# Which FFN chunks are turned by VectorE and DMA, and which by TensorE: three and ten instead of nine and nine

## The chip, the core and the metric

The kernel runs on one core of one Trainium2 chip. The metric is the device time of one execution in microseconds (us). Before the change the median of three runs is 1899.93 us (1897.19 to 1902.32). Engines are named as in the profile: PE is the matrix engine (PEld its weight loads), DVE the vector engine, ACT the scalar engine, POOL the general engine, SP the engine whose queue issues most loads.

## What is computed

A decoder trunk of two layers over 256 tokens with 2048 features, all in 32-bit floats. Layer 0 mixes tokens by causal pooling, layer 1 by latent attention; each layer ends with a gated feed-forward network (FFN) with 5632 inner features. What matters here:

```python
def swiglu(h, w_gate, w_up, w_down):
    return (jax.nn.silu(h @ w_gate) * (h @ w_up)) @ w_down
...
        x = x + gate_m[:, None, :] * y
        h = modulate(rmsnorm(x, norm_ffn[i]), shift_f, scale_f)
        x = x + gate_f[:, None, :] * swiglu(h, ffn_gate[i], ffn_up[i], ffn_down[i])
```

## The kernel before

**Units.** Every weight matrix is cut into units of 512 by 512 (1 MB). A unit is loaded by SP into one of six `raw` buffers (L389), split by ACT into a rounded upper half (`hi`, L376) and by DVE into the rest (`lo = raw - hi`, L378), and multiplied by PE in 24 matmuls of 128x512 (L422): `hi` by both halves of the activations, `lo` by the upper half, for four slices of 128 rows and two tiles of 128 tokens. The halves lie in six `hl` buffers, so PE can be at most three units behind the splits. Matmuls accumulate in eight PSUM banks.

**An FFN.** The inner features are eleven chunks of 512. `project_chunk(c)` (p in the list below) multiplies the hidden state by the gate and up columns of chunk c; ACT takes the silu (L852), DVE multiplies (L856) into `nat[c]`, two tiles with tokens on the partitions. For the down projection the features of the chunk must lie on the partitions: `transposed(c)` (t) turns `nat[c]` into `mids[c]`, again as upper and lower half. `down(i)` (d) multiplies a group of two or three chunks by their rows of `w_down`. The order is written out by hand:

```python
FFN_STEPS = "p0 p1 t0 p2 t1 p3 t2 p4 p5 d0 t3 t4 p6 t5 d1 p7 t6 p8 t7 p9 t8 d2 p10 t9 d3".split()
GROUPS = ([0, 1, 2], [3, 4, 5], [6, 7, 8], [9, 10])
```

Three quarters of the gate and up products of chunks 0 to 5 are made ahead of these steps (`start_ffn`); their sums lie in SBUF, and DVE adds the last quarter from PSUM (L722).

**Two ways of turning.** A chunk below `TURNED_BY_DMA` = 9 is turned in blocks of 32: DVE turns 32x32 blocks within the tile (`turn_blocks`, L752), POOL writes the tile to DRAM (L754, 256 KB), `transposed` lets POOL read it back with the blocks in their places (L769), and then ACT and DVE make the halves from SBUF (`turned_halves`, L761 and L762). The rows of `w_down` are stored in the order that this leaves. A chunk from 9 on is turned by PE: four 128x128 transposes into a PSUM bank for each token tile (L777), and ACT and DVE make the halves from PSUM (L780, L781). In the last group the transposes of chunk 10 are issued inside the first unit of d3.

**Background.** During the first FFN, DVE also sums the modulation vectors of later stages: tiles of 1 MB are loaded into the same six `raw` buffers (L212) and reduced by DVE (L213), by a rate of about one tile per unit. When the sixteen tiles of one vector are summed, DVE writes the column (L302), and PE turns it (L294) for the gate of the FFN.

**Order on the engines.** A scheduler sets it when the program is built, from the order of the code and priorities (the splits stand a little ahead). On each engine instructions run in the order that it set, and an instruction that waits holds back what stands behind it. `pending` holds work that is issued in code order a unit or two later, behind the next splits.

Of the kernel before, what the change touches and what calls it, by code (L numbers as in the profile page):

```python
# [17 lines left out]
P = 128  # L18
# [4 lines left out]
CH = 512  # L23
ND = D // CH
F = 5632
NF = F // CH
DEPTH = 2
# [6 lines left out]
KL = LORA // P  # L34
# [23 lines left out]
FFN_STEPS = "p0 p1 t0 p2 t1 p3 t2 p4 p5 d0 t3 t4 p6 t5 d1 p7 t6 p8 t7 p9 t8 d2 p10 t9 d3".split()  # L58
GROUPS = ([0, 1, 2], [3, 4, 5], [6, 7, 8], [9, 10])
BLOCK = 32  # L60
TURNED_BY_DMA = 9

BEGUN = 6
ASIDE = 5
# [31 lines left out]
def tile_trunk(ctx: ExitStack, tc: tile.TileContext, a: dict, out: bass.AP):  # L96
# [19 lines left out]
    def act_t(shape, dt=F32R):  # L116
        return work.tile(shape, dt, tag="act", bufs=8, name=nm("act"))

    def t2k(shape, dt=F32):
        return work.tile(shape, dt, tag="t2k", bufs=7, name=nm("t2k"))  # L120
# [7 lines left out]
    def ps_t():  # L128
        return psum.tile([P, CH], F32, tag="ps", name=nm("ps"))
# [143 lines left out]
    pending = []  # L273
# [329 lines left out]
    def stream_aside(l):  # L603
        if l == 0:
            return
        aside[l] = dram.tile([P, NT, D], F32, name=nm("aside"))
        with tc.issue_after(w_load[0].ins):
            sync.dma_start(aside[l], x)
# [129 lines left out]
    def ffn(l, hT, gate_name, begun, then):  # L738
# [3 lines left out]
        def project(c, which):  # L742
            if c in begun:
                begun[c][which].block(ND - 1, hT[ND - 1])
                return begun[c][which].result()
            return proj(ffn_weights(l)[which][:, c], hT)

        def turn_blocks(c):
            turned[c] = []
            for tok in range(NT):  # L750
                blocks = t2k([P, CH])
                dve.transpose(out=blocks, in_=nat[c][tok])  # L752
                rows = dram.tile([P, CH], F32, name=nm("turned"))
                pool.dma_start(rows, blocks)  # L754
                turned[c].append(rows)

        def turned_halves(m, tok, full):
            order = "p k (b j) -> p k b j"
            v = full.rearrange("p (b k j) -> p k b j", k=KL, j=BLOCK)
            upper, lower = (m[:, i, :, tok * P:(tok + 1) * P].rearrange(order, j=BLOCK) for i in range(2))  # L760
            act.activation(upper, v, AF.Copy)  # L761
            dve.tensor_tensor(out=lower, in0=v, in1=upper.bitcast(F32), op=ALU.subtract)  # L762

        def transposed(c):
            m = act_t([P, 2, KL, T])
            if c < TURNED_BY_DMA:
                for tok in range(NT):
                    full = t2k([P, CH])
                    pool.dma_start(full.rearrange("p (b e) -> p b e", e=P),  # L769
                                   turned[c][tok].rearrange("(b i) (g e) -> (i g) b e", i=BLOCK, e=P))  # L770
                    pending.append((1, lambda tok=tok, full=full: turned_halves(m, tok, full)))
                mids[c] = m
                return
            for tok in range(NT):
                pt = ps_t()
                for f in range(KL):
                    pe.transpose(pt[:, f * P:(f + 1) * P], nat[c][tok][:, f * P:(f + 1) * P], ident)  # L777
                v = pt.rearrange("p (f t) -> p f t", f=KL)
                ts_ = slice(tok * P, (tok + 1) * P)
                act.activation(m[:, 0, :, ts_], v, AF.Copy)  # L780
                dve.tensor_tensor(out=m[:, 1, :, ts_], in0=v, in1=m[:, 0, :, ts_].bitcast(F32), op=ALU.subtract)  # L781
            mids[c] = m
# [9 lines left out]
        def down(i):  # L792
# [6 lines left out]
            for j in range(ND):  # L799
# [29 lines left out]
                for c in g:  # L829
                    hi, lo = w_unit(wd[c, j])  # L830
                    turning = last and j == 0 and c == g[0]
                    proj_unit(banks, mids[c], hi, lo, c == g[0], c == g[-1],
                              between=(lambda: transposed(g[-1])) if turning else None)
# [6 lines left out]
        def project_chunk(c):  # L840
            if c == ASIDE:
                stream_aside(l)
            if c == NF - 1:
                end = StreamEnd(l)
                stream_end.append(end)
                for n, wait in enumerate(KNOWN):
                    pending.append((wait, lambda n=n: end.known(n // NT, n % NT, gates[gate_name])))
            gb = project(c, GATE)
            nat[c] = []
            for tok in range(NT):  # L850
                sg = t2k([P, CH])
                pending.append((0, lambda sg=sg, bank=gb[tok]: act.activation(sg, bank, AF.Silu)))  # L852
                nat[c].append(sg)
            ub = project(c, UP)
            for tok in range(NT):
                dve.tensor_tensor(out=nat[c][tok], in0=ub[tok], in1=nat[c][tok], op=ALU.mult)  # L856
            if c < TURNED_BY_DMA:
                pending.append((0, lambda: turn_blocks(c)))

        for step in FFN_STEPS:  # L860
            {"p": project_chunk, "t": transposed, "d": down}[step[0]](int(step[1:]))
# [845 lines left out]
def units(w):  # L1707

    k, n = w.shape
    w = w.reshape(k // CH, KL, P, n // CH, CH).transpose(0, 3, 2, 1, 4)  # L1710
    return w.reshape(k // CH, n // CH, P, KL * CH)


def laid_out(i):

    def columns(v):
        return np.asarray(v).reshape(-1, P).T

    o = {n: np.asarray(i[n]) for n in ("x", "c", "positions", "mod_w", "final_norm")}
    o["vectors"] = np.concatenate([columns(i[n]) for n in (  # L1720
        "c", "norm_mix", "norm_ffn", "kv_in_norm", "kv_norm", "q_norm", "pool_scale", "mod_b", "kv_mod_b")], 1)
    o["mod_wt"] = o["mod_w"].transpose(0, 2, 1)
    o["kv_mod_wt"] = np.asarray(i["kv_mod_w"]).T
    block = o["mod_w"][0].reshape(KD // 2, 2, P, 6, D)[:, :, :, 3:5, :CH]
    o["mod_block"] = block.transpose(0, 2, 1, 3, 4).reshape(KD // 2, P, 4 * CH)

    w = np.asarray(i["w_uq"])[0].reshape(KL, P, H // 2, 2, QH)
    rope = w[..., NOPE:].reshape(KL, P, H // 2, 2, 2, HALF).swapaxes(3, 4).reshape(KL, P, H // 2, 2 * ROPE)
    w = np.concatenate([rope, w[..., :NOPE].reshape(KL, P, H // 2, 2 * NOPE)], 3)
    o["w_uq"] = w.transpose(2, 1, 0, 3).reshape(H // 2, P, -1)  # L1730
    w = np.asarray(i["w_kr"]).reshape(KD, P, 2, 1, HALF)
    o["w_kr"] = np.concatenate([w, w], 3).reshape(KD, P, P).transpose(1, 0, 2).reshape(P, KD * P)
    for n in ("w_dkv", "w_uk", "w_uv"):
        o[n] = units(np.asarray(i[n]))
    o["pool_w"] = np.asarray(i["pool_w"])[0].reshape(-1, KL, P, CH).transpose(0, 2, 1, 3).reshape(-1, P, KL * CH)
    for n in ("w_dq", "w_o"):
        o[n] = units(np.asarray(i[n])[0])
    for n in ("ffn_gate", "ffn_up", "ffn_down"):
        o[n] = np.stack([units(w) for w in np.asarray(i[n])])
    w = np.asarray(i["ffn_down"]).reshape(DEPTH, NF, KL, KL, BLOCK, ND, CH)[:, :TURNED_BY_DMA]  # L1740
    o["ffn_down"][:, :TURNED_BY_DMA] = w.transpose(0, 1, 5, 4, 2, 3, 6).reshape(DEPTH, TURNED_BY_DMA, ND, P, KL * CH)
    return o


# [16 lines left out]
```

## Time and the profile before

| | |
|---|---|
| median of three runs | 1899.93 us (1897.19 to 1902.32) |
| profiled execution | 1897.58 us, span 1895.8 us |
| mean granted clock of PE | 0.992 |
| PE busy | 1833.5 us (97% of the span) |
| DVE busy | 1437.9 us (76%) |
| ACT busy | 835.9 us (44%) |
| DMA of SP's queue | 570.68 MB, 77.5% of 16 engines |
| DMA of POOL's queue | 22.02 MB, 3.1% of 16 engines |

The parts of the span, by PE's rows: the modulation vectors and the pooling mixer until 166 us, the first FFN until about 888 us (its `start_ffn` until about 362 us), the attention until about 1174 us, the last FFN to the end (1895.8 us). The span is counted from the first instruction to the last of the profiled execution; its own time is 1.8 us longer. A row of the timeline gives the start, the length, the engine, the line, the operation and, in brackets, how long the engine had been idle and what ended that.

### The profile page before, as it was taken

To read this page: it belongs to the slowest core of one execution; us is meant where nothing else is said; L and a number is where in the kernel's file an instruction comes from. 1 tells how busy PE (TensorE), PEld (TensorE's weight loads), DVE (VectorE), ACT (ScalarE), POOL (GpSimd) and SP (SyncE) were. 2 spreads that over 40 slices of the span, in tenths; PEclk is the share of its full clock that TensorE was granted. 3 is DMA by queue.
4 is the path that set the end of the run, shared out by engine and by line. 5 is a ranking of instruction groups with operands and counts; after the bars stand their busy time and mean duration, and the time that the engine had idled before them with its cause. 6 is when DMAs were issued, how large, how long until landed. Compare 5 with 4: busy or idle time off the path is not lost.

```text
span 1895.8 us, 21717 instructions
## 1 busy us (share of the span) xinstructions
PE 1833.5 (97%) x8589; PEld 1485.8 (78%) x8589; DVE 1437.9 (76%) x1447; ACT 835.9 (44%) x914; POOL 69.1 (4%) x102
## 2 busy tenths in 40 slices
PE   6689999998999999999999999999999999999998
PEld 2356888886888888888889888888888888888886
DVE  1248799999889798997798886889788666644557
ACT  3125643443443343344766635634444433344343
POOL 0000000010000000000100000000011000000000
PEclk9989999999999999999999999999999999999999
DMA  9999998899999899995494485989788776765551
GB/s 398 417 420 415 387 363 338 317 356 349 410 401 417 356 398 395 390 420 223 181 381 171 159 351 191 397 323 331 264 312 326 285 270 236 273 250 207 218 200 45
DMA packets 85879, 594.37 MB, mean 314 GB/s; under 512 B 10081, under 2 KB 10513, under 8 KB 17041
## 3 DMA queue, kind: packets, MB, share of 16 engines
q1 hardware_dynamic: 79346, 570.68, 77.5%
q0 software_dynamic: 6192, 22.02, 3.1%
q8 instruction: 67, 1.10, 0.2%
q10 hardware_dynamic: 240, 0.29, 0.0%
q14 instruction: 34, 0.28, 0.0%
HBM read 577.20 MB, written 15.75 MB: 313 GB/s over the span
## 4 chain that ended last, share of the span: by engine, by line
PE 88%; DMA 7%; DVE 3%; issue 1%; ACT 1%; SPq 0%; POOLq 0%; DVEq 0%; ACTq 0%
PE ps L422 76%; DMA raw<-in_mod_w_dram 6%; PE ps L431 2%; PE ps L1382 1%; DVE hl L378 1%; PE ps L258 1%; PE ps L1029 1%; PE ps L1468 1%; PE ps L1574 1%; DVE raw L213 1%; DMA raw<-in_ffn_down_dram 1%; PE ps L1285 1%; ACT hl L376 0%; DMA raw<-in_mod_block_dram 0%; PE ps L564 0%
## 5 line engine op out<-in xcount | busy, mean ns | idle before, releaser
L422 PE MATMUL ps<-hl,act 128*128 128x512 f32 x6672 | 1520.5, 390 | 4.1 <-ACT hl L376 3.3
L422 PEld LDWEIGHTS ps<-hl,act 128*128 128x128 f32 x6672 | 1252.5, 188 | 265.6 <-ACT hl L376 4.4
L376 ACT ACTIVATE hl<-raw 128x2048 fp32r<-128x2048 f32 x285 | 546.1, 1917 | 671.0 <-PE ps L422 397.1
L378 DVE TENSOR_TENSOR hl<-raw,hl 128x2048 fp32r<-128x2048 f32 x285 | 651.3, 2287 | 200.9 <-ACT hl L376 198.9
L213 DVE SCALAR_TENSOR_TENSOR raw<-raw,s_row 128x2048 f32<-128x2048 f32 x168 | 383.0, 2284 | 12.9 <-DMA raw<-in_mod_wt_dram 12.1
L258 PE MATMUL ps<-raw,s_strip 128*32 128x512 f32 x392 | 58.9, 686 | 39.3 <-DMA raw<-in_mod_w_dram 38.1
L722 DVE TENSOR_TENSOR act<-ps,act 128x512 f32<-128x512 f32 x96 | 63.8, 681 | 14.7 <-PE ps L422 14.7
L258 PEld LDWEIGHTS ps<-raw,s_strip 128*32 128x32 f32 x392 | 8.9, 116 | 69.6 <-DMA raw<-in_mod_w_dram 48.7
L754 POOL DMA_DIRECT2D turned<-t2k x36 | 20.1, 561 | 800.3 <-DVE t2k L752 799.9
L431 PE MATMUL ps<-hl,act 128*128 128x512 f32 x192 | 47.6, 400 | 0.6 <-DVE act L527 0.5
L431 PEld LDWEIGHTS ps<-hl,act 128*128 128x128 f32 x192 | 35.1, 188 | 10.3 <-ACT act L514 2.5
L790 DVE TENSOR_TENSOR x<-ps,x 128x512 f32<-128x512 f32 x32 | 21.5, 688 | 19.9 <-PE ps L422 19.9
L769 POOL DMA_DIRECT2D t2k<-turned x36 | 27.5, 764 | 222.1 <-issue 106.2
L544 DVE TENSOR_TENSOR hl<-raw,hl 128x2048 fp32r<-128x2048 f32 (+3 forms) x17 | 31.9, 1879 | 4.8 <-ACT hl L541 4.7
L265 DVE COPY t2k<-ps 128x256 f32<-128x256 f32 x4 | 1.7, 424 | 44.0 <-ACT t2k L264 44.0
L856 DVE TENSOR_TENSOR t2k<-ps,t2k 128x512 f32<-128x512 f32 x24 | 16.5, 688 | 23.6 <-PE ps L422 23.6
L1029 PEld LDWEIGHTS ps<-act,act 128*128 128x128 f32 x128 | 24.0, 194 | 11.3 <-issue 8.4
L451 ACT ACTIVATE junk<-x 128x512 bf16<-128x512 f32 x23 | 14.4, 628 | 41.0 <-DVE x L636 23.9
L720 ACT ACTIVATE act<-ps 128x512 f32<-128x512 f32 x32 | 19.1, 596 | 29.0 <-PE ps L422 29.0
L1029 PE MATMUL ps<-act,act 128*128 128x256 f32 x128 | 30.9, 392 | 0.0
L752 DVE STREAM_TRANSPOSE t2k<-t2k 128x512 f32<-128x512 f32 x36 | 24.3, 695 | 7.3 <-DMA turned<-t2k 7.1
L852 ACT ACTIVATE t2k<-ps 128x512 f32<-128x512 f32 x24 | 14.2, 591 | 35.1 <-PE ps L422 35.1
(235 smaller groups left out, 1024.7 us busy)
## 6 DMA issues: line engine op xcount, KB each, us to landing
raw<-in_mod_wt_dram SPq DMA_DIRECT2D x136, 1024.0 KB, 7.0
raw<-in_ffn_up_dram SPq DMA_DIRECT2D x88, 1024.0 KB, 6.4
raw<-in_ffn_down_dram SPq DMA_DIRECT2D x88, 1024.0 KB, 7.1
raw<-in_ffn_gate_dram SPq DMA_DIRECT2D x87, 1024.0 KB, 6.4
raw<-in_mod_w_dram SPq DMA_DIRECT2D x48, 1024.0 KB, 13.8
raw<-in_kv_mod_wt_dram SPq DMA_DIRECT2D x32, 1024.0 KB, 10.3
raw<-in_w_o_dram SPq DMA_DIRECT2D x16, 1024.0 KB, 6.6
turned<-t2k POOLq DMA_DIRECT2D x36, 256.0 KB, 5.9
```

What stands on the lines that cost most here:

```text
L213: dve.scalar_tensor_tensor(out=r, in0=r, scalar=1.0, in1=s_row, op0=ALU.mult, op1=ALU.mult, accum_out=self.sums[:, self.n:self.n + 1])
L258: pe.matmul(self.bank[m * STRIP:(m + 1) * STRIP, :], lhsT=weights(k), rhs=r[:, k, i, :], start=first, stop=last)
L376: hi_ins = act.activation(hi, r, AF.Copy)
L378: lo_ins = dve.tensor_tensor(out=lo, in0=r, in1=hi.bitcast(F32), op=ALU.subtract)
L422: pe.matmul(banks[tok], lhsT=t_[:, i, k, tok * P:(tok + 1) * P], rhs=w[:, k, :], start=first and n < len(part), stop=last and n >= len(ord ...
L431: pe.matmul(bank, lhsT=t_[:, i, k, tok * P:(tok + 1) * P], rhs=w[:, k, :], start=first and n == 0, stop=last and n == len(order) - 1)
L544: dve.tensor_tensor(out=w[2][:, ks], in0=w[0][:, ks], in1=w[1][:, ks].bitcast(F32), op=ALU.subtract)
L722: dve.tensor_tensor(out=part, in0=banks[tok], in1=part, op=ALU.add)
L752: dve.transpose(out=blocks, in_=nat[c][tok])
L769: pool.dma_start(full.rearrange("p (b e) -> p b e", e=P), turned[c][tok].rearrange("(b i) (g e) -> (i g) b e", i=BLOCK, e=P))
L790: dve.tensor_tensor(out=sums, in0=bank, in1=sums, op=ALU.add)
L1029: pe.matmul(mixed[g][:, n % 2, :], lhsT=wp[g][:, k, ns], rhs=pool_all[g // 2][:, g % 2, k, :], start=k == 0, stop=k == KL - 1)
```

## The change

`TURNED_BY_DMA` becomes one range for each FFN. In the first FFN only chunks 6, 7 and 8 are turned by VectorE and DMA; chunks 0 to 5 join 9 and 10 on PE. In the last FFN chunks 0 to 9 are turned by VectorE and DMA; only chunk 10 stays on PE. For chunk 9 the halves are issued where the read back is issued, without going through `pending`, since `d3` follows at once. The stored order of the rows of `w_down` follows the same ranges.

```diff
-TURNED_BY_DMA = 9
+TURNED_BY_DMA = (range(6, 9), range(10))
...
         def transposed(c):
             m = act_t([P, 2, KL, T])
-            if c < TURNED_BY_DMA:
+            if c in TURNED_BY_DMA[l]:
                 for tok in range(NT):
                     full = t2k([P, CH])
                     pool.dma_start(full.rearrange("p (b e) -> p b e", e=P),
                                    turned[c][tok].rearrange("(b i) (g e) -> (i g) b e", i=BLOCK, e=P))
-                    pending.append((1, lambda tok=tok, full=full: turned_halves(m, tok, full)))
+                    halves = lambda tok=tok, full=full: turned_halves(m, tok, full)
+                    if c == GROUPS[-1][0]:
+                        halves()
+                    else:
+                        pending.append((1, halves))
                 mids[c] = m
                 return
...
-            if c < TURNED_BY_DMA:
+            if c in TURNED_BY_DMA[l]:
                 pending.append((0, lambda: turn_blocks(c)))
```

Lines behind the edit have numbers up to five higher in the changed kernel: the transposes are L781 there, their halves L784 and L785, DVE's multiplication is L860.

**First place: DVE in the first FFN, at chunk 2** (`t2k_2517` and `t2k_2507` are its `nat`, `act_2463` and `act_2455` the turned chunk 0, `raw_2...` with `s_row` is a tile of the background). Before:

```order
L378 TENSOR_TENSOR hl_2624<-raw_2618,hl_2623 128x2048
L722 TENSOR_TENSOR act_960<-ps_2520,act_960 128x512
L856 TENSOR_TENSOR t2k_2517<-act_960,t2k_2517 128x512
L856 TENSOR_TENSOR t2k_2518<-act_960,t2k_2518 128x512
L213 SCALAR_TENSOR_TENSOR raw_2569,sums_2339<-raw_2569,s_row 128x2048
L762 TENSOR_TENSOR act_2463<-t2k_2464,act_2463 128x4x128
L762 TENSOR_TENSOR act_2463<-t2k_2466,act_2463 128x4x128
L378 TENSOR_TENSOR hl_2670<-raw_2664,hl_2669 128x2048
L752 STREAM_TRANSPOSE t2k_2576<-t2k_2517 128x512
L752 STREAM_TRANSPOSE t2k_2580<-t2k_2518 128x512
```

The same place after the change:

```order
L378 TENSOR_TENSOR hl_2612<-raw_2606,hl_2611 128x2048
L722 TENSOR_TENSOR act_960<-ps_2509,act_960 128x512
L213 SCALAR_TENSOR_TENSOR raw_2608,sums_2339<-raw_2608,s_row 128x2048
L722 TENSOR_TENSOR act_960<-ps_2510,act_960 128x512
L860 TENSOR_TENSOR t2k_2507<-act_960,t2k_2507 128x512
L860 TENSOR_TENSOR t2k_2508<-act_960,t2k_2508 128x512
L378 TENSOR_TENSOR hl_2668<-raw_2662,hl_2667 128x2048
L785 TENSOR_TENSOR act_2455<-ps_2456,act_2455 128x4x128
L785 TENSOR_TENSOR act_2455<-ps_2463,act_2455 128x4x128
```

The two block transposes of each chunk are gone from DVE; the halves of chunk 0 are made at about the same place, from PSUM. From the split of `hl_2527` (now `hl_2517`, the same unit: the second of p2) to L302, which ends the sum that PE's L294 waits for, both counted, DVE had 14 splits (L378), 12 background tiles, 19 additions (L722), 10 multiplications, 10 block transposes and 6 lower halves of turned chunks; now it has 12, 12, 18, 10, none and 6.

**Second place: PE in the first FFN, at the end of p1** (`ps_2415` belongs to the second unit of p1, `ps_2470` to the first of p2, `ps_2456` and `ps_2463` are the banks of turned chunk 0). Before, p2 follows p1 at once:

```order
L422 MATMUL ps_2423<-hl_2429,act_2256 128x512 x8
L422 MATMUL ps_2423<-hl_2430,act_2256 128x512 x4
L422 MATMUL ps_2468<-hl_2475,act_2256 128x512 x8
L422 MATMUL ps_2468<-hl_2476,act_2256 128x512 x4
L422 MATMUL ps_2469<-hl_2475,act_2256 128x512 x8
```

After:

```order
L422 MATMUL ps_2415<-hl_2421,act_2256 128x512 x8
L422 MATMUL ps_2415<-hl_2422,act_2256 128x512 x4
L781 MATMUL ps_2456<-con,t2k_2335 128x128 x4
L781 MATMUL ps_2463<-con,t2k_2336 128x128 x4
L422 MATMUL ps_2470<-hl_2477,act_2256 128x512 x8
L422 MATMUL ps_2470<-hl_2478,act_2256 128x512 x4
```

Eight transposes stand between p1 and p2, behind 960 unit matmuls of the first FFN. Those of chunks 1 and 2 follow behind p2 and p3; those of chunks 3, 4 and 5 stand late in d0 and in d1. PE's L294 stood behind 1296 unit matmuls and stands behind 1272 now.

**Third place: PE at the start of d3 in the last FFN** (`ps_12781` and `ps_12788` are the banks of chunk 9, `ps_12823` and `ps_12830` those of chunk 10, `hl_12802` and `hl_12792` the upper half of d3's first unit). Before:

```order
L422 MATMUL ps_12651<-hl_12749,act_9691 128x512 x4
L777 MATMUL ps_12781<-con,t2k_12005 128x128 x4
L777 MATMUL ps_12788<-con,t2k_12006 128x128 x4
L422 MATMUL ps_12798<-hl_12802,act_12780 128x512 x3
L422 MATMUL ps_12799<-hl_12802,act_12780 128x512 x3
L422 MATMUL ps_12798<-hl_12802,act_12780 128x512
L422 MATMUL ps_12799<-hl_12802,act_12780 128x512
L777 MATMUL ps_12823<-con,t2k_12648 128x128 x4
L777 MATMUL ps_12830<-con,t2k_12649 128x128 x2
```

After, the unit's first sixteen matmuls follow the last unit of p10 directly, and only the transposes of chunk 10 are left:

```order
L422 MATMUL ps_12647<-hl_12745,act_9679 128x512 x4
L422 MATMUL ps_12788<-hl_12792,act_12776 128x512
L422 MATMUL ps_12789<-hl_12792,act_12776 128x512
...
L781 MATMUL ps_12813<-con,t2k_12644 128x128 x4
L781 MATMUL ps_12820<-con,t2k_12645 128x128 x4
L422 MATMUL ps_12788<-hl_12793,act_12776 128x512
```

Chunk 9 takes the way through POOL instead; on POOL its two reads (`t2k_12777`, `t2k_12781`) stand right behind its two writes, and nothing but the end of the kernel stands behind them:

```order
L754 DMA turned_12136<-t2k_12134 128x512
L754 DMA turned_12140<-t2k_12138 128x512
L769 DMA t2k_12777<-turned_12136 128x4x128
L769 DMA t2k_12781<-turned_12140 128x4x128
L597 TENSOR_TENSOR sm_13071<-sm_13073,mhalf 128x1
```

More of the change, by code (lines that the diff above doesn't have):

```diff
@@ L1739, in laid_out @@
         o[n] = np.stack([units(w) for w in np.asarray(i[n])])
-    w = np.asarray(i["ffn_down"]).reshape(DEPTH, NF, KL, KL, BLOCK, ND, CH)[:, :TURNED_BY_DMA]
-    o["ffn_down"][:, :TURNED_BY_DMA] = w.transpose(0, 1, 5, 4, 2, 3, 6).reshape(DEPTH, TURNED_BY_DMA, ND, P, KL * CH)
+    for l, chunks in enumerate(TURNED_BY_DMA):
+        w = np.asarray(i["ffn_down"])[l].reshape(NF, KL, KL, BLOCK, ND, CH)[list(chunks)]
+        o["ffn_down"][l, list(chunks)] = w.transpose(0, 4, 3, 1, 2, 5).reshape(len(chunks), ND, P, KL * CH)
     return o
```

## The prediction, made before the changed kernel ran

> **What bounds the kernel now.** I read the chain of work that ended last first, then the table by stretches, then who PE waits for.
>
> ```profile
> PE 88%; DMA 7%; DVE 3%; issue 1%; ACT 1%; SPq 0%; POOLq 0%; DVEq 0%; ACTq 0%
> 166.29 218.03 PE ps L422 x960
> 469.88 0.38 PE ps L294
> 470.26 366.88 PE ps L422 x1608
> 837.14 0.87 PE ps L777 x8
> ```
>
> The chain is PE's for 88% of the span, and inside the FFNs it is one run of unit matmuls after another. So each transpose added to PE is paid in full, and time can be won only where PE stands idle. Between 384.32 us (the end of the first run quoted) and 470.26 us the chain leaves PE. The stretches show it:
>
> ```profile
> core 0: us, PE busy (x) PEld busy (x) DVE busy (x) ACT busy (x) POOL busy (x), PEclk, DMA share, GB/s
> 166.00:384.00 218.00, 217.97 (x963) 180.04 (x962) 195.73 (x185) 103.22 (x96) 1.97 (x4) 1.00 0.93 357
> 384.00:470.00 86.00, 77.28 (x340) 62.88 (x338) 81.71 (x83) 34.75 (x32) 12.18 (x19) 0.99 0.94 351
> 470.00:837.00 367.00, 367.00 (x1610) 303.48 (x1610) 324.13 (x251) 142.68 (x94) 10.76 (x16) 0.99 0.99 398
> PE ps L294 <- DVE cols L302: 5.4, 1, 5.4
> PE ps L422 <- ACT hl L376: 3.3, 2, 2.4
> ```
>
> From 384 to 470 us PE is idle for 86.00 - 77.28 = 8.7 us, all of it in three waits (the last two rows, 5.4 + 3.3), while DVE is busy for 81.71 of 86. Everywhere else in the first FFN PE is full. This is where the chunks 0 to 5 are turned. The idle time has an echo, seen in slices of 3 us (columns: PE busy with its count, granted clock, DMA share, GB/s):
>
> ```profile
> 456.00:459.00 3.00, 0.64 (x3) 1.00 1.02 400
> 468.00:471.00 3.00, 1.12 (x4) 0.52 1.03 429
> 471.00:474.00 3.00, 3.00 (x9) 0.50 1.05 412
> 474.00:477.00 3.00, 3.00 (x13) 0.84 0.97 385
> 477.00:480.00 3.00, 3.00 (x15) 1.00 1.03 429
> ```
>
> After the wait of 5.4 us the granted clock was about half until some point in 474 to 477, and PE made 9 and 13 matmuls where 15 fit. The wait of 2.4 us (in 456 to 459) left the clock at 1.00. The whole loss of this stage: from 384.32 to 837.14 are 452.8 us for 336 + 1608 = 1944 unit matmuls (the counts by the order); at 218.03 / 960 = 0.2271 us each they need 441.5, L294 0.4. So 10.9 us are lost: 8.7 idle, 2.2 by the slow clock.
>
> **Why DVE is late there.** Rows of DVE in order of time, which give its pitch, start to start, and the group of its splits from 384 to 470 us (count, busy us and mean ns, idle before them and what ended it):
>
> ```profile
> 378.51 2.27 DVE L213 SCALAR_TENSOR_TENSOR raw<-raw,s_row 128x2048 f32<-128x2048 f32 x1
> 380.71 2.29 DVE L378 TENSOR_TENSOR hl<-raw,hl 128x2048 fp32r<-128x2048 f32 x1
> 382.91 2.12 DVE L722 TENSOR_TENSOR gate<-ps,gate 128x512 f32<-128x512 f32 x3
> 384.95 1.29 DVE L856 TENSOR_TENSOR t2k<-gate,t2k 128x512 f32<-128x512 f32 x2
> 386.15 0.70 DVE L752 STREAM_TRANSPOSE t2k<-t2k 128x512 f32<-128x512 f32 x1
> 469.66 0.17 DVE L302 TENSOR_TENSOR cols<-sums,vcol 128x16 f32<-128x16 f32 x1
> L378 DVE TENSOR_TENSOR hl<-raw,hl 128x2048 fp32r<-128x2048 f32 x13 | 29.6, 2275 | 4.1 <-ACT hl L376 4.0
> ```
>
> A split costs 2.20, a background tile 2.28 with its readout, a 512-wide operation 0.60 (two L856 in 1.20). From 380.71 to the end of L302 at 469.83 the order has 14 splits, 12 tiles, 45 narrow operations (10 of them block transposes) and L302: 30.8 + 27.4 + 27.0 + 0.1 = 85.3 us, and with the 4.0 us in which splits waited for ACT 89.3, against 89.1 by the clock: the count explains the stretch. PE without waits would reach L294 at 166.29 + 1296 x 0.2271 = 460.6 us, so L302 is 9.2 us late.
>
> **The change, first FFN.** From the same split to L302 the new order has 12 splits, 12 tiles, 34 narrow operations and L302: 26.4 + 27.4 + 20.4 + 0.1 = 74.3 us, so L302 ends at 455.0. PE reaches L294 behind 1272 matmuls and three groups of eight transposes: 166.29 + 288.9 + 2.6 = 457.8. DVE is 2.8 us early instead of 9.2 late. Of this swing of 12.0 us, 6.6 are eleven narrow operations, 4.4 the two splits that now stand behind L302, 3.8 the waits for ACT, and 2.8 go off since PE comes earlier. The same count gives the unit before L294 its lower half at 452.6, where PE, at the unit from 452.3 on, wants it behind sixteen matmuls, at 456. I take the 8.7 us of waits and the 2.2 of clock as gone.
>
> The cover of this is loading. Each unit needs its load, then ACT's split, then DVE. The rows of loads are for 380 to 520 us (count, size, us from issue to landing; the queue's last number is its share of DMA time); those of ACT, of the whole span, give the mean ns before the second bar.
>
> ```profile
> L376 ACT ACTIVATE hl<-raw 128x2048 fp32r<-128x2048 f32 x285 | 546.1, 1917 | 671.0 <-PE ps L422 397.1
> L780 ACT ACTIVATE act<-ps 128x512 fp32r<-128x512 f32 x8 | 4.4, 590 | 8.0 <-PE ps L777 8.0
> L761 ACT ACTIVATE act<-t2k 128x512 fp32r<-128x512 f32 x36 | 20.3, 618 | 21.0 <-issue 11.4 <-DVE t2k L856 9.6
> raw<-in_ffn_down_dram SPq DMA_DIRECT2D x12, 1024.0 KB, 8.3
> raw<-in_kv_mod_wt_dram SPq DMA_DIRECT2D x12, 1024.0 KB, 11.2
> t2k<-turned POOLq DMA_DIRECT2D x12, 256.0 KB, 7.0
> turned<-t2k POOLq DMA_DIRECT2D x10, 256.0 KB, 6.0
> q0 software_dynamic: 2058, 7.34, 13.6%
> ```
>
> POOL's queue took 13.6% of all DMA time, 19 us of 140, nearly all of it for turning; that goes. What stays, two tiles of 1 MB a unit, is 2.1 MB each 5.45 us or 385 GB/s, where slices show up to 429. Loads are issued as DVE frees buffers, so an earlier DVE also loads earlier. I cost loading at nothing; if the cover fails, the late part is `hi` from ACT for the units of d0, at most the 10.9 us of now. Bounds: 0 and 10.9 us left over; I take 0, as 470 to 837 has PE full at a DMA share of 0.99.
>
> On PE six chunks by eight transposes are added. The nearest rows are those of chunk 9, which stands between unit matmuls just so:
>
> ```profile
> 836.98 1.04 PE L777 MATMUL ps<-con,t2k 128*128 128x128 f32 x8
> L777 PE MATMUL ps<-con,t2k x32: 270/272/273, 837.0 to 1846.8; 128*128 128x128 f32 x32
> ```
>
> Eight take 0.87 us of the chain, 0.109 each, though one record lasts 272 ns: they overlap. Six groups are 5.2 us, all on the path; PE is full there. Nothing makes them wait: by the same count `nat` of chunks 0, 1 and 2 is ready at about 374, 391 and 400 us, where PE arrives at 384, 396 and 408, and their banks are freed by L722 and L785 some 5 us ahead of their next users. ACT makes an upper half from PSUM in 590 ns, from SBUF in 618, and DVE has as many lower halves as before. First FFN: -10.9 + 5.2 = -5.7 us.
>
> The Trainium skill, "TensorE: Matmul & The Clock Gate", "Part 4: PE-mode transpose", measured about 275 ns for one transpose inside a kernel and says that transposes do not count as busy for the clock. If 275 ns were the pitch, 48 would be 13.2 us. The row's 272 ns agrees as a length, and the chain's 0.109 speaks against it as a pitch. The same page, "Part 1: The HAM clock gate", lets an idle window of about 3.4 us halve the clock. The trace agrees (5.4 us did, 2.4 did not).
>
> **The change, last FFN.** Rows of PE and of what chunk 9 needs:
>
> ```profile
> 1835.77 4.93 PE L422 MATMUL ps<-hl,act 128*128 128x512 f32 x21
> 1840.54 1.04 PE L777 MATMUL ps<-con,t2k 128*128 128x128 f32 x8
> 1842.28 2.11 PE L422 MATMUL ps<-hl,act 128*128 128x512 f32 x8 [0.69 <-ACT act L780]
> 1844.23 0.82 PE L777 MATMUL ps<-con,t2k 128*128 128x128 f32 x6
> 1731.93 0.69 DVE L856 TENSOR_TENSOR t2k<-ps,t2k 128x512 f32<-128x512 f32 x1 [1.21 <-PE ps L422]
> turned<-t2k POOLq DMA_DIRECT2D x36, 256.0 KB, 5.9
> t2k<-turned POOLq DMA_DIRECT2D x36, 256.0 KB, 6.7
> ```
>
> Between the last matmul of p10 (1840.70) and the first of d3 (1842.28) lie the eight transposes of chunk 9 and 0.69 us of waiting for ACT: 1.58 us, which go. Those of chunk 10 cost the same at their new place, behind sixteen matmuls. Chunk 9 is multiplied by 1732.6; block transposes 1.2, write 5.9 and read 6.7 bring it back before 1750, some 90 us ahead. DVE gets 1.2 us more in a stretch where it waits for PE: nothing. Last FFN: -1.6 us.
>
> **Sum.** -5.7 - 1.6 = -7.3 us. The profiled execution took 1897.58 us (span 1895.8 and 1.8 around it), so 1890.3; it lies 2.4 below the median of 1899.93, which gives **1892.6 us**.
>
> **Rivals.**
> *Part of the wait stays.* For: L302 is early by 2.8 us only, less than the 3.8 of waits for ACT that I dropped, and loads of the background took 11.2 us to land. Against: the DMA time freed. If half the idle time stays, 4.4 us in waits too short to slow the clock, the gain is 2.9: 1897.0.
> *The change does not do what it says:* loads, not DVE, held this stage, since ACT waited for them, so the 10.9 us stay. Then +5.2 - 1.6: 1903.5. Against: the count of DVE explains the stretch to 0.2 us.
> *Transposes at 0.272 us,* each on the path (the skill's figure, above, gives the same): 48 cost 13.1, so 13.1 - 10.9 - 1.6 = +0.6: 1900.5. Against: 0.87 for eight.
> *Slower: chunk 9 comes back late.* d3 begins with it, and ACT and DVE wait for it in order, with the splits of p10 behind them. If the whole round trip began where PE needs it: block transposes 1.2, landings 5.9 and 6.7, halves 0.6 and 0.6, 15.0 us, and 2.2 of slow clock: +17.2 - 7.3, 1909.8. It decides from 5 us of waiting on. Against: the reads stand right behind the writes on POOL, and the buffers they take were last used near 1732.
>
> **How the numbers follow.** Forecast 0.63; part of the wait stays 0.18; loads hold it 0.07; dear transposes 0.05; chunk 9 late 0.03; more gain than counted 0.04. A difference of 0.3%, 5.7 us, is about what a measurement of this kernel can tell from none. The forecast lies only 1.6 us beyond that, and medians of three scatter by some 2 us; so of its 0.63 about 0.53 are faster, with the last case 0.57. Same: 0.10 of the forecast, 0.17 of the second, 0.05 and 0.05 of the next two, 0.37. Slower 0.06. The forecast's own range is 1889.5 to 1895.5; to hold 8 in 10 I reach to 1888 and to 1899.5.
>
> **What the profile after would show.** No wait of PE at L294, PE full from 166 to 888 us, no slice at half clock near 470; PE's transposes in groups of 0.87 us; L302 at about 455; POOL's queue lighter by 20 transfers; d3 starting on p10's last matmul. Wrong would be: waits of PE for `hi` between 440 and 480, transposes above 0.2 us each in the chain, or ACT waiting for chunk 9's read in p10.

## The result, and the profile after

The changed kernel took 1889.84 us (median of six runs, 1889.67 to 1892.37); the kernel before, beside it, 1898.8 us (1896.53 to 1902.32). The ratio is 0.9955, with a 95% interval of 0.9942 to 0.9968: faster by 0.45%. 1892.6 was forecast, with 1888.0 to 1899.5 as the range. Execution against execution, the profiled ones took 1897.58 and 1889.67 us: 7.9 us less, where the sum said 7.3.

The chain of waits of the changed kernel (start, length, what):

```profile
PE 93%; DMA 5%; DVE 0%; ACT 0%; SPq 0%; issue 0%; POOLq 0%; DVEq 0%; ACTq 0%
166.76 218.00 PE ps L422 x960
384.75 0.87 PE ps L781 x8
...
409.21 48.98 PE ps L422 x216
458.19 0.11 PE ps L294
458.29 27.26 PE ps L422 x120
485.55 0.87 PE ps L781 x8
...
526.29 304.81 PE ps L422 x1344
...
881.84 9.98 PE ps L431 x44
...
1144.74 9.98 PE ps L431 x44
...
1839.16 34.55 PE ps L422 x152
1873.71 5.76 PE ps L828 x48
```

The chain no longer leaves PE between 384 and 470 us. The added transposes stand in it as groups of 0.87 us. The group at 525.42 is that of chunk 5: by the counts above 1560 unit matmuls are ahead of it, and d0 ends behind 1440 and p6 behind 1632, so it stands in p6, and not in d1 as said above. The same points in the chain of the kernel before:

```profile
887.88 9.98 PE ps L431 x44
1150.78 9.98 PE ps L431 x44
...
1881.58 5.76 PE ps L824 x48
```

From the first unit matmul to the first L431 (the end of the first FFN) it took 887.88 - 166.29 = 721.6 us before and 881.84 - 166.76 = 715.1 now: 6.5 less. From the second of these L431 rows to the last matmuls (L824, now L828) it took 730.8 before and 729.0 now: 1.8 less. In between both took 262.9, and the first FFN began 0.5 later in this execution, in a part that waits for loads of `mod_block`. -6.5 - 1.8 + 0.5 and a few hundredths in the tail make the 7.9.

The stretches and one of the slices:

```profile
core 0: us, PE busy (x) PEld busy (x) DVE busy (x) ACT busy (x) POOL busy (x), PEclk, DMA share, GB/s
384.00:470.00 86.00, 86.00 (x394) 71.32 (x393) 82.94 (x77) 39.19 (x34) 0.71 (x1) 1.00 0.87 335
470.00:837.00 367.00, 367.00 (x1636) 304.04 (x1635) 321.50 (x253) 141.00 (x94) 7.95 (x12) 1.00 0.97 391
468.00:471.00 3.00, 3.00 (x15) 2.49 (x14) 3.00 (x4) 0.54 (x1) 0.00 (x0) 1.00 1.01 421
```

PE is busy for all of the 86.00 us, where it was for 77.28, and the granted clock from 468 to 471 us is 1.00 with fifteen matmuls, where it was 0.52 with four. DVE is as busy as before (82.94 against 81.71), with other work: by its groups in this stretch 14 splits and 15 background tiles, where it had 13, 13 and ten block transposes. The DMA share fell from 0.94 to 0.87.

Rows of DVE and PE around L302 and L294, and of PE at d3:

```profile
380.57 2.28 DVE L378 TENSOR_TENSOR hl<-raw,hl 128x2048 fp32r<-128x2048 f32 x1
454.80 0.18 DVE L302 TENSOR_TENSOR cols<-sums,vcol 128x16 f32<-128x16 f32 x1
461.02 2.29 DVE L378 TENSOR_TENSOR hl<-raw,hl 128x2048 fp32r<-128x2048 f32 x1 [1.61 <-ACT hl L376]
458.02 0.27 PE L294 MATMUL ps<-con,cols 128*16 128x128 f32 x1
1838.12 1.04 PE L781 MATMUL ps<-con,t2k 128*128 128x128 f32 x8
1838.92 11.45 PE L422 MATMUL ps<-hl,act 128*128 128x512 f32 x49
```

L302 ends at 454.98 (forecast 455.0), and PE comes to L294 at 458.0 (forecast 457.8) without a wait. DVE waits 1.61 us for ACT behind L302, and no wait of PE follows from it. At d3 no bracket with a wait is left; the eight transposes of chunk 10 follow matmuls of d3. The second read of chunk 9 was issued at 1736.40 us, and ACT made the upper halves at 1814.32 and 1818.38, without a wait, ahead of d3.

### The profile page after: what moved, and what is told of

It reads as the page before. It is cut to its first block, busy times and chain, and to the rows that moved or that the text cites. A ratio compares the mean times of both kernels' runs of the same rounds, so it can differ in the third digit from the quotient of the medians.

```text
span 1887.9 us, 21743 instructions
## 1 busy us (share of the span) xinstructions
PE 1836.0 (97%) x8629; PEld 1489.2 (79%) x8629; DVE 1431.6 (76%) x1437; ACT 836.2 (44%) x914; POOL 56.1 (3%) x82
## 4 chain that ended last, share of the span: by engine, by line
PE 93%; DMA 5%; DVE 0%; ACT 0%; SPq 0%; issue 0%; POOLq 0%; DVEq 0%; ACTq 0%
PE ps L422 80%; DMA raw<-in_mod_w_dram 5%; PE ps L431 2%; PE ps L1033 2%; PE ps L1386 1%; PE ps L258 1%; PE ps L1472 1%; PE ps L1578 1%; PE ps L1289 1%; PE ps L781 0%; PE ps L564 0%; PE ps L1475 0%; DMA raw<-in_mod_block_dram 0%; PE ps L1487 0%; PE ps L1527 0%; PE ps L1488 0%
## 5 line engine op out<-in xcount | busy, mean ns | idle before, releaser
L378 DVE TENSOR_TENSOR hl<-raw,hl 128x2048 fp32r<-128x2048 f32 x285 | 651.3, 2287 | 196.6 <-ACT hl L376 196.5
L722 DVE TENSOR_TENSOR act<-ps,act 128x512 f32<-128x512 f32 x96 | 63.9, 682 | 15.4 <-PE ps L422 15.4
L431 PE MATMUL ps<-hl,act 128*128 128x512 f32 x192 | 47.6, 400 | 0.6 <-DVE act L527 0.5
L431 PEld LDWEIGHTS ps<-hl,act 128*128 128x128 f32 x192 | 35.1, 188 | 10.3 <-ACT act L514 2.5
L1033 PEld LDWEIGHTS ps<-act,act 128*128 128x128 f32 x128 | 25.0, 202 | 11.7 <-issue 8.4
L754 POOL DMA_DIRECT2D turned<-t2k x26 | 14.5, 556 | 649.6 <-DVE t2k L752 649.3
L860 DVE TENSOR_TENSOR t2k<-ps,t2k 128x512 f32<-128x512 f32 x24 | 16.5, 687 | 19.9 <-PE ps L422 19.9
L541 ACT ACTIVATE hl<-raw 128x2048 fp32r<-128x2048 f32 (+1 forms) x15 | 26.5, 1766 | 3.5 <-PE ps L422 3.5
```

What stands on the lines that cost most here:

```text
L378: lo_ins = dve.tensor_tensor(out=lo, in0=r, in1=hi.bitcast(F32), op=ALU.subtract)
L431: pe.matmul(bank, lhsT=t_[:, i, k, tok * P:(tok + 1) * P], rhs=w[:, k, :], start=first and n == 0, stop=last and n == len(order) - 1)
L541: hid_ins[0] = act.activation(w[1], w[0], AF.Copy)
L722: dve.tensor_tensor(out=part, in0=banks[tok], in1=part, op=ALU.add)
L1033: pe.matmul(mixed[g][:, n % 2, :], lhsT=wp[g][:, k, ns], rhs=pool_all[g // 2][:, g % 2, k, :], start=k == 0, stop=k == KL - 1)
```

## The experiments

All of them ran beside the kernel before. "First FFN" is the time from the first unit matmul to the first L431 of the chain, from one profiled execution each; it resolves tenths of a us, which the medians don't. In ffn0_only, ffn1_only, both_kept, blocks_copies and best6 the FFN begins at half clock (the last section comes back to this), ahead of anything the edits touch: by their first 960 matmuls that is 0.3 to 1.7 us of the last column.

| kernel | median us | ratio to before (95%) | first FFN us |
|---|---|---|---|
| before | 1897.2 to 1898.8 | 1 | 721.6 |
| changed | 1889.84 | 0.9955 (0.9942 to 0.9968) | 715.1 |
| ffn0_only | 1892.14 | 0.9967 (0.9954 to 0.9980) | 716.8 |
| ffn1_only | 1896.88 | 0.9996 (0.9988 to 1.0005) | 722.8 |
| blocks_kept | 1893.89 | 0.9975 (0.9965 to 0.9984) | 719.5 |
| traffic_kept | 1890.93 | 0.9963 (0.9950 to 0.9977) | 715.1 |
| both_kept | 1903.37 | 1.0031 (1.0020 to 1.0042) | 729.7 |
| blocks_copies | 1904.39 | 1.0038 (1.0026 to 1.0051) | 729.3 |
| held6 | 1902.73 | 1.0022 (1.0014 to 1.0031) | 725.5 |
| best6 | 1901.65 | 1.0016 (1.0006 to 1.0025) | 725.8 |
| ffn1_all_pe | 1899.72 | 1.0009 (1.0000 to 1.0018) | 715.1 |
| from5_9 | 1888.57 | 0.9954 (0.9941 to 0.9966) | 714.4 |
| from4_9 | 1889.75 | 0.9957 (0.9943 to 0.9970) | 716.8 |
| from5 | 1889.88 | 0.9952 (0.9934 to 0.9971) | 714.2 |

The first four runs take the change apart.

**ffn0_only: the part in the first FFN alone.**

```diff
-TURNED_BY_DMA = (range(6, 9), range(10))
+TURNED_BY_DMA = (range(6, 9), range(9))
```

> The first FFN as in the changed kernel, the last FFN as before (chunk 9 turned by PE again). My theory, by the chains of the two traces (first FFN 721.6 us before and 715.1 after): 6.5 us less than before, no wait of PE between 384 and 470 us, L302 at about 455, and the 0.7 us wait of d3 for ACT back; 1.8 us more than the changed kernel. Rival, that the two parts help each other (a lighter queue of POOL): a gain that differs from 6.5 by 2 us or more.

The trace has no wait of PE in the first FFN and the 0.7 us for ACT at d3. From the second L431 to the last matmuls it takes 730.8 us, as before. By the medians it gains 5.8 us, within its interval of the 6.5. The first FFN is 716.8 in the profiled execution, for its slow start; from the end of the first 960 matmuls to the first L431 it takes 497.0 us, and the changed kernel 497.1.

**ffn1_only: the part in the last FFN alone.**

```diff
-TURNED_BY_DMA = (range(6, 9), range(10))
+TURNED_BY_DMA = (range(9), range(10))
```

> The last FFN as in the changed kernel, the first as before. My theory: 1.8 us less than before (eight transposes 0.87, the wait 0.69, and the slower first eight matmuls behind it 0.27); the waits of 5.4 us at L294 and of 3.3 us for ACT stay and the half clock near 470 us with them. Rival, that most of the gain of 9 us by the medians is of the last FFN: 4 us or more.

```profile
PE ps L294 <- DVE cols L302: 4.7, 1, 4.7
PE ps L422 <- ACT hl L376: 4.6, 4, 2.1
```

The waits of the first FFN are there again (4.7 + 4.6 against 5.4 + 3.3 us). From the second L431 row of its chain (1153.75) to the last matmuls (1882.71) it takes 729.0 us, 1.8 less than before. The ratio's interval, from 2.3 us less to 0.9 more, takes in both 1.8 and nothing. So most of the gain is of the first FFN, and the two parts add.

**blocks_kept: DVE's block transposes without POOL's transfers.** In `project_chunk`, of the changed kernel:

```diff
             if c in TURNED_BY_DMA[l]:
                 pending.append((0, lambda: turn_blocks(c)))
+            elif l == 0 and c < 6:
+                def blocks_alone():
+                    for tok in range(NT):
+                        dve.transpose(out=t2k([P, CH]), in_=nat[c][tok])
+                pending.append((0, blocks_alone))
```

> The changed kernel, but DVE still makes the two block transposes of each of the chunks 0 to 5 in the first FFN; nothing reads them, and POOL moves nothing for them. PE has its 48 transposes. My theory (DVE's count made PE wait): from the same split to L302 the order has 14 splits, 12 tiles and 45 narrow operations again, 85.3 us, so L302 at 466.5 or, with the 4 us of waits for ACT, 470, against PE at L294 at 463.1: a wait of 3 to 7 us at L294, half clock behind it if it is over 3.4, so 3 to 9 us more than the changed kernel. Rival (the transfers of POOL's queue made the loads late, and with them the splits): no wait, the time of the changed kernel within 1 us.

```profile
380.55 2.28 DVE L378 TENSOR_TENSOR hl<-raw,hl 128x2048 fp32r<-128x2048 f32 x1
465.47 0.17 DVE L302 TENSOR_TENSOR cols<-sums,vcol 128x16 f32<-128x16 f32 x1
454.69 8.32 PE L422 MATMUL ps<-hl,act 128*128 128x512 f32 x36
465.70 0.28 PE L294 MATMUL ps<-con,cols 128*16 128x128 f32 x1 [2.69 <-DVE cols L302]
L378 DVE TENSOR_TENSOR hl<-raw,hl 128x2048 fp32r<-128x2048 f32 x14 | 32.0, 2283 | 0.0
```

The wait at L294 is back: PE is there at 463.0 and L302 ends at 465.64. From the split at 380.55 these are 85.1 us, against 85.3 by the count, and the last row (splits from 384 to 470 us; behind the last bar the idle time before them) has no wait for ACT at all. So the block transposes on DVE are a cause by themselves, by the count. They cost the first FFN 4.4 us, more than the 2.7 of the wait; the slow clock behind it is shown at the end. But L302 is not at 469.8 as in the kernel before, since the 4.0 us in which splits waited for ACT are missing; the next run shows what they go with.

**traffic_kept: POOL's transfers without DVE's block transposes.**

```diff
+            elif l == 0 and c < 6:
+                def write_alone():
+                    turned[c] = []
+                    for tok in range(NT):
+                        rows = dram.tile([P, CH], F32, name=nm("turned"))
+                        pool.dma_start(rows, nat[c][tok])
+                        turned[c].append(rows)
+                pending.append((0, write_alone))
```

and in `transposed`, ahead of the transposes by PE, `pool.dma_start` of these rows into two fresh `t2k` tiles.

> The changed kernel, but POOL still writes the chunks 0 to 5 of the first FFN to DRAM and reads them back, into tiles that nothing reads; DVE has no block transposes for them. My theory: no wait of PE between 384 and 470, the time of the changed kernel within 1 us. Rival (the transfers): PE waits for the upper halves between 440 and 470 as before, up to 11 us more than the changed kernel.

```profile
384.00:470.00 86.00, 86.00 (x393) 71.36 (x392) 82.95 (x77) 39.02 (x34) 10.64 (x17) 1.00 0.99 382
470.00:837.00 367.00, 367.00 (x1636) 304.03 (x1636) 321.99 (x253) 142.34 (x95) 11.75 (x17) 1.00 0.98 397
```

The DMA share of the stage went up to 0.99, above the 0.94 of the kernel before, and PE stays full. The first FFN takes what it takes in the changed kernel. Transfers alone cost nothing; my cover held. The loads do land later with them, as the loads of `w_down` from 380 to 470 us show (count, size, median us from issue to landing) in the kernel before, in blocks_kept and in traffic_kept:

```profile
raw<-in_ffn_down_dram SPq DMA_DIRECT2D x9, 1024.0 KB, 7.4
raw<-in_ffn_down_dram SPq DMA_DIRECT2D x10, 1024.0 KB, 5.3
raw<-in_ffn_down_dram SPq DMA_DIRECT2D x11, 1024.0 KB, 9.2
```

With DVE's block transposes a load took 7.4 us beside POOL's transfers and 5.3 without them; without the block transposes it took 9.2 beside them and 7.1 in the changed kernel, which has none there. So the transfers go with some 2.1 us in both pairs. Yet no split of traffic_kept waits for ACT ahead of L302 (at 454.44), and none of blocks_kept does. Of these four kernels only the kernel before, with late loads and the block transposes on DVE together, has the 4.0 us of such waits.

**both_kept and blocks_copies: both together.** The first has block transposes, writes and reads, as two edits above with `turn_blocks`; in the second the read goes from DRAM to DRAM:

```diff
+            if l == 0 and c < 6:
+                for tok in range(NT):
+                    pool.dma_start(dram.tile([P, KL, P], F32, name=nm("junk")),
+                                   turned[c][tok].rearrange("(b i) (g e) -> (i g) b e", i=BLOCK, e=P))
```

> The changed kernel, but for the chunks 0 to 5 of the first FFN DVE still makes the block transposes and POOL writes and reads them, into tiles that nothing reads: all the work of before, with 48 transposes of PE more. The block transposes alone cost the first FFN 4.4 us (719.5 against 715.1 us), the transfers alone nothing (715.05). If the two only add, it is 4.4 us more than the changed kernel. My theory now: they do not add; late loads hold DVE's splits only where DVE has no slack left, so L302 is at 469.8 as before, PE comes to L294 at 463.1, and 6.7 us of waits and 2 us of slow clock make about 8.5 us more than the changed kernel.

> Again block transposes by DVE and transfers by POOL for the chunks 0 to 5 beside the 48 transposes of PE, but what POOL reads back goes from DRAM to DRAM and takes no tile, since both_kept held two tiles a chunk more than the kernel before and its chain runs over waits for tiles (DVE and ACT for POOL's transfers). Additive: the first FFN takes 719.5 us as with the block transposes alone, 4.4 more than the changed kernel. My theory (late loads hold the splits only where DVE has no slack): L302 at 469 to 470 as in the kernel before instead of 465.5, PE at L294 at 463.1, some 6.5 us of waits and 2 of slow clock: a first FFN of about 723.5 us, 8.5 more than the changed kernel.

Both cost about 14 us in the first FFN (13 to 13.5 behind the slow start), far over my 8.5. The chain of blocks_copies says why it can't be read as the sum of two causes:

```profile
437.75 9.41 DMA turned<-t2k
...
447.25 0.04 ACT t2k L860
...
447.79 1.90 ACT hl L376
...
456.36 6.60 DMA turned<-t2k
...
463.06 0.16 DVE t2k L752
```

A silu of ACT (its line is L860 here) needs a `t2k` tile and gets it when POOL's write of an older one has landed; `hi` of the next unit stands behind it on ACT, so the split is late, and at 463.06 a block transpose of DVE waits for a tile in the same way. In these two kernels `nat` is held until PE has turned it, beside the tiles that POOL writes, and seven tiles are not enough. In the kernel before the chain runs at this place over loads, not over POOL's writes:

```profile
435.15 7.92 DMA raw<-in_ffn_down_dram
...
450.83 5.88 DMA raw<-in_ffn_down_dram
```

What is shown: blocks alone 4.4 us, transfers alone 0. The change took 6.5 + 5.2 = 11.7 us off the first FFN ahead of the price of its 48 transposes, so some 7.3 us were there only with both. That they are the late loads meeting a late DVE is argued from the waits and the landings; no run has the two together without running short of tiles.

**held6: the turning of before, but less background in this stage.** In the kernel before, behind `plan(n_all + MIX_LATE, FFN0_UNITS)`:

```diff
+    credit[0] = -6.0
+    rate[0] *= FFN0_UNITS / (FFN0_UNITS - 6)
```

> The kernel before with its turning unchanged, but the background of the first FFN begins six units later (no tile for the first six units of these steps, then a rate higher by 87/81), so DVE has some six tiles of 2.28 us less in p0 to p5 and the loads 6 MB less. My theory (DVE has too much work in this stage, whatever kind it is): the waits between 384 and 470 us and the half clock are gone without any transpose on PE, the first FFN takes 710 us instead of 721.6, and the kernel 11 us less than before. Rival (what helps is only that block transposes leave DVE or POOL's queue): waits of 5 us or more stay. Another: the tiles come back as waits of PE between 500 and 880 us.

```profile
384.00:470.00 86.00, 84.26 (x368) 68.40 (x368) 80.65 (x81) 36.25 (x32) 11.63 (x18) 1.00 0.91 337
470.00:600.00 130.00, 125.27 (x541) 101.74 (x540) 115.63 (x90) 50.80 (x36) 5.48 (x8) 0.99 1.01 407
600.00:837.00 237.00, 233.34 (x1025) 191.68 (x1024) 210.64 (x166) 87.97 (x56) 5.31 (x8) 1.00 0.98 399
PE ps L422 <- ACT hl L376: 4.6, 3, 2.9
PE ps L422 <- DVE hl L378: 3.6, 4, 2.1
```

(The last two rows are PE's waits from 470 to 888 us.) The wait at L294 is gone (its sum is finished later here: L302 is at 484.84, and PE comes to L294 at 486.14), and PE's idle time in the stage fell from 8.7 to 1.7 us, without a transpose on PE. But the tiles came back as 8.4 us of idle time from 470 to 837 us, as the last rival has it, and the first FFN takes 3.9 us more than before. From 470 to 600 us the DMA share is 1.01 and 407 GB/s, so a load that was not made ahead of 470 us found no room there. I read this as an FFN that is short of loading as a whole and of DVE in one place. Work moved in time did not help; DVE's block transposes taken away did, by traffic_kept even with the transfers left in.

**best6: all but chunk 10 by DVE and DMA, with the background held as in held6.** `TURNED_BY_DMA = (range(10), range(10))` and the two lines above.

> All chunks but chunk 10 turned by DVE and DMA in both FFNs, and the background held back by six units as in held6. Against the changed kernel 56 transposes of PE less in the first FFN, 7 groups of 0.87 us: if DVE has room without the six tiles, no wait between 384 and 470, a first FFN of 708.9 us instead of 715.1, and about 6 us less than the changed kernel, 1883.7 us. If the stage is still too full: a wait at L294 of some us and about the changed kernel's time. If chunk 9 of the first FFN comes back late for d3: a wait of PE near 830 us.

No wait at L294, but 10.6 us of PE's waits from 384 to 888 us (6.4 for ACT, 4.2 for DVE), all but 0.9 of them between 470 and 837 us, where the DMA share is 1.00: the 6 us did not come, and it is slower than the kernel before.

**ffn1_all_pe: what eight transposes cost.** `TURNED_BY_DMA = (range(6, 9), range(0))`.

> The changed kernel, but the last FFN turns all eleven chunks by PE: ten groups of eight transposes more. By the pitch of the chain (0.87 us for eight) and the start of d3 as before (0.7 of waiting, 0.3 of slow start): 8.7 + 1.0 = 9.7 us more than the changed kernel. By the length of a record, 0.272 us each on the path: 21.8 + 1.0 = 22.8 us more. PE is full between the groups there, so a transpose that overlaps less beside other work would show as a group of more than 0.9 us in the chain.

```profile
1144.03 9.98 PE ps L431 x44
...
1732.22 0.87 PE ps L781 x8
...
1882.80 5.76 PE ps L828 x48
```

From the second L431 to the last matmuls 738.8 us, against 729.0 in the changed kernel: 9.8 more, where 9.7 were worked out by the pitch and 22.8 by the length of a record. The medians, which were not taken beside each other, differ by 9.9. Each group stands in the chain with 0.87 us.

**Three ways to turn a chunk or two less on PE.** `TURNED_BY_DMA` for the first FFN as `range(5, 10)`, `range(4, 10)` and `range(5, 9)`.

> The changed kernel, but of the first FFN also chunks 5 and 9 turned by DVE and DMA (chunks 5 to 9). Two groups of eight transposes less on PE: 1.75 us. Ledger of DVE to L302: two narrow operations more than the changed kernel, so 456.1 instead of 454.9, PE there at 457.9: no wait. So 1.7 us less than the changed kernel, a first FFN of 713.3 us. Rival: the two transfers of chunk 5, in the stretch with a DMA share of 0.97, make loads late, with waits of PE for ACT between 480 and 600 us, and the time is that of the changed kernel or more.

> As before it, but chunks 4 to 9 of the first FFN turned by DVE and DMA. Three groups of eight transposes less on PE than the changed kernel, 2.6 us. The order has 13 splits, 12 tiles and 38 narrow operations to L302: 78.9 us, L302 at 459.6 to 460, and PE at L294 at 460.4: by the count just no wait, 2.6 us less than the changed kernel. Rival: with nothing to spare late loads hold the splits again, 2 to 5 us of waits for ACT or at L294 and perhaps half clock, so the same as the changed kernel or up to 3 us more.

> The changed kernel, but of the first FFN also chunk 5 turned by DVE and DMA, and chunk 9 left on PE: what from5_9 did at chunk 5 alone. In from5_9 PE waited 0.8 us for a lower half at 750 us and ran without a wait until then; chunk 9's block transposes stand at 742 us, in a stretch with a DMA share of 0.99. My theory: chunk 9 brought that wait, so here there is none, the first FFN takes 715.1 - 0.87 = 714.2 us, and the kernel 0.9 us less than the changed kernel, which its median can hardly tell. Rival: chunk 5's transfers made the loads late for good, and the wait near 750 us stays.

The first gave 0.6 us of its 1.7 in the trace: PE waited 0.8 us at 750 us for a lower half. The second lost 1.7: PE waited 1.9 us for ACT and 0.8 for DVE, with L302 at 460.12 and L294 at 460.56, by the count just without a wait. These 2.7 us eat up the 2.6 that three groups save; a good part of the rest is the slower start behind each of the four waits (one run of 24 matmuls took 5.78 us there, where 24 at 0.2268 are 5.44).

```profile
751.17 99.37 PE L422 MATMUL ps<-hl,act 128*128 128x512 f32 x437 [0.83 <-DVE hl L378]
460.12 0.17 DVE L302 TENSOR_TENSOR cols<-sums,vcol 128x16 f32<-128x16 f32 x1
460.56 0.27 PE L294 MATMUL ps<-con,cols 128*16 128x128 f32 x1
```

(The first row is PE's in from5_9, the other two are of from4_9.) The third has no wait of PE and takes 714.2 us in the first FFN, 0.9 less than the changed kernel, as expected: chunk 9, not chunk 5, brought the wait at 750 us. Its median (1889.88) can't tell that from nothing; no version tried is measurably faster than the changed kernel.

## Why the prediction was right, and which steps were off

- *PE's idle time between 384 and 470 us and the slow clock behind it go.* Shown: 8.7 us of waits are 0, and no slice of 3 us in the first FFN is below 1.00. The first FFN gained 0.8 us more than forecast (6.5 against 5.7). The step that was mis-sized is the price of a matmul: 0.2271 us by the first 960, where the run of 1344 in the trace after has 304.81 / 1344 = 0.2268. On the 1944 matmuls of the stage that is 0.6 us, so the loss was nearer 11.5 than 10.9; L294 also takes 0.11 in the chain (its row above), where it took 0.38. -11.5 - 0.3 + 5.2 is -6.6.
- *DVE's count sets L302.* Right in time, to 0.1 us, and blocks_kept confirms the count by itself. One part of it came right without a term of its own: I dropped the 3.8 us of waits for ACT, and of the two things that the change takes away either would have done. blocks_kept, whose DVE has all the work of before and no transfers, has none of them; traffic_kept, with the transfers and no block transposes, has none ahead of L302. The transfers were a part of the loss before, then, though alone they cost PE nothing.
- *Loading costs nothing.* Held in the changed kernel, with a share of 0.87 and 0.97. But I took the full DMA of 470 to 837 us as a sign of cover; held6 and best6 have waits there, at shares of 1.00 and 1.01, so it is nearer a limit, and the cover is thin: three chunks back on DVE and DMA (from4_9) cost 1.7 us net, and two (from5_9) gave a third of what they save on PE.
- *Eight transposes 0.87 us, all on the path.* Shown in the chain of the changed kernel and again, times ten, in ffn1_all_pe. The Trainium skill, "TensorE: Matmul & The Clock Gate", "Part 4: PE-mode transpose", has about 275 ns for one; these runs agree with that as a length and not as a pitch.
- *Last FFN.* 1.8 instead of 1.6 us: behind the wait the first eight matmuls took 2.11 us, and eight at 0.2268 are 1.81; the missing 0.3 were in the row that I quoted, and I did not count them. Chunk 9 came back in time, as counted.
- *The forecast of 1892.6* is 2.8 over the median because I added 2.4 us for the distance of one execution to a median of three. Six runs of before have 1898.8 as their median; the execution itself was off by 0.6 us.

Of the rivals, none took place here: no part of the wait stayed, the loads did not hold the stage, transposes were not dear, and chunk 9 was not late.

## What to carry to other kernels

When an engine that is full on average waits in one stage, count the instructions of the engine that feeds it there, from the order, and compare the sum with its clock time: the count gave L302 to 0.1 us. Then take work off that engine (here DVE's block transposes, for 0.87 us of PE a chunk: traffic_kept shows that this alone brought the whole gain of the first FFN). Moving work to a later stage helps only if that stage has room; here it had none (held6). A full DMA queue alone is not the sign: at a share of 0.99 traffic_kept has no wait of PE. Price a short operation by its share of the chain, not by the length of its record.

## What the runs showed of the hardware

The granted clock fell after a wait of 2.69 us, where in the kernel before a wait of 2.4 us had left it at 1.00. The slices of blocks_kept around that wait, which ended at 465.70:

```profile
462.00:465.00 3.00, 1.01 (x5) 0.51 (x3) 3.00 (x3) 0.60 (x1) 0.00 (x0) 1.00 0.96 344
465.00:468.00 3.00, 2.30 (x7) 1.81 (x8) 3.00 (x5) 1.56 (x2) 0.00 (x0) 0.66 1.01 410
468.00:471.00 3.00, 3.00 (x12) 2.43 (x11) 3.00 (x3) 1.51 (x2) 0.00 (x0) 0.78 1.03 431
```

The granted clock was 0.66 and 0.78 in two slices. The Trainium skill, "TensorE: Matmul & The Clock Gate", "Part 1: The HAM clock gate", names an idle window of about 3.4 us; no 3.4 us without a matmul are seen here. The length of a wait does not decide it alone in these runs. Ahead of the first FFN, from 159 to 166 us, PE has the same three waits in the kernel before and in ffn0_only (0.56, 1.09 and 0.56 us). The eight transposes behind them (L1072, in ffn0_only L1076):

```profile
165.19 1.07 PE L1072 MATMUL ps<-con,x 128*128 128x128 f32 x8
165.54 1.95 PE L1076 MATMUL ps<-con,x 128*128 128x128 f32 x8
```

From 166 to 170 us the granted clock was 1.00 in the first and 0.50 in the second. So the same short waits cost nothing in one execution and 1.7 us of slow matmuls (in the first 960) in another. What the gate looks at, these runs do not tell.
